# Two-part weights of a mixer kept in DRAM by its first block, and elementwise work moved from GpSimd to VectorE

## The chip, the core and the metric

The kernel runs on one core of a Trainium2 chip. Its engines work side by side: TensorE (PE in the rows; PEld is its weight load) multiplies, VectorE (DVE), ScalarE (ACT) and GpSimd (POOL) work elementwise, SyncE (SP) issues all DMA transfers of this kernel from one queue, in order, and 16 DMA engines carry them out. The metric is device time of one execution in microseconds. Before the change the median of three runs is 2590.94 us (2590.84 to 2595.94).

## What is computed

One layer of a streaming encoder on 2048 tokens of width 1024, in float32. Cut to what matters:

```python
def _token_mixer(xn, w_in, ..., w_out):
    p = einsum('btd,de->bte', xn, w_in)
    gB, gC, hA = split(p[..., :3 * CONV_DIM], 3)
    y_a = gC * _causal_dwconv(gB * hA, conv_a_w)
    ...                                # r, k, v, decay, gate of a delta-rule state
    y = _wkv7(r4, d4, k4, v4, kk, a4)  # chunks of 64 tokens, one after the other
    ...
    return einsum('bte,ed->btd', concatenate([y_a, y_b]), w_out)

def _channel_mixer(hn, w_up, ffn_conv_w, ffn_conv_b, w_down):
    f = einsum('btd,df->btf', hn, w_up)
    f = _causal_dwconv(f, ffn_conv_w) + ffn_conv_b
    gate, up = split(f, 2)
    return einsum('btf,fd->btd', gelu(gate) * up, w_down)

h = x + rms_norm(_token_mixer(rms_norm(x, pre_mix_g), ...), post_mix_g)
out = h + rms_norm(_channel_mixer(rms_norm(h, pre_ffn_g), ...), post_ffn_g)
```

## The kernel before

The 2048 tokens are four blocks of 512. **Operands in two parts.** TensorE multiplies in float32r, so every weight and every activation is split into a high part (`hi`, a cast by ScalarE) and a low part (`lo = src - hi`, a subtraction by VectorE): `split`, line 483. A product is three matmuls, high by high, high by low, low by high. `gemm` (line 490) does that for one output tile of 128 columns: it takes the weights in pieces of 128x512 (256 KB, four 128-row tiles, 12 matmuls), loads a piece into the ring `wraw` (three buffers), and splits it into the rings `whi` and `wlo` (three buffers each). Half of an input projection of 1024 rows is one piece.

**Mixer weights met four times.** The input weights `w_in` are used by all four blocks. For them `gemm` gets a name `keep`: block 0 computes both parts and stores the low one to DRAM (`lower`), blocks 1 to 3 load the raw piece, cast `hi` again on ScalarE, and load `lo`. In block 0 the low part of the second piece (k0 = 4) is computed by GpSimd (`pool_e if keep and k0 else dve`). This holds for 26 projections, 52 pieces. The output weights `w_out` (8 tiles, 16 pieces) are split anew in each of the four calls of `out_proj` (line 599), on ScalarE and VectorE.

**Stages.** The mixer blocks 0 to 3 (each a plan of its own) mix projections with the chain of the 64-token state; block b also does `out_proj(b-1)` and `residual`. Then one plan holds the rest: `out_proj(3)`; `up(0)` for blocks 0 and 1 (22 pairs of tiles, seven half-size products each, after Strassen's scheme, in `up_pair`), where `up_weights` also forms four sums of weight quarters and stores them (`s_d`); `down_block(0)` and `down_block(1)`; `up(1)` for blocks 2 and 3, which loads the stored sums; `down_block(2)` and `(3)`. Of the four sums, s1 and s3 (`wu0s`, `wu2s`) run on GpSimd, s2 and s4 (`wu1s`) on VectorE.

**Other GpSimd work.** In block 0 `short_conv` multiplies by the late norm factor (`u`, `cv`). At the end of each down block `finish` (line 1497) scales the eight tiles `fo` by the norm factor and adds the residual `ho` to them: tiles 0 to 2 are scaled and tiles 0 and 1 added by GpSimd, which needs a copy `rb` of the factor that ScalarE takes out of PSUM; VectorE does the others, straight from PSUM (`rps`). `ho` has two buffers, so tile 2 is loaded when tile 0 has been stored. The operand `t4` of `up(1)` lies in the places of `fo` (slots 48 to 55), so its last part is written when `finish(1)` is through.

**What sets the order.** Nothing runs in the order of the code. The code records operations into a `Plan`, which schedules them as a list, engine by engine, by costs of its own (`Plan.cost`, a price for each kind of operation, engine and width) over 16 rounds, and then emits them; on the chip each engine and the one DMA queue keep that order. All instructions are recorded by one helper, so the profile gives line 431 for all, and one goes by tile names.

## Time and profile before

| | us |
|---|---|
| median of three runs | 2590.94 |
| lowest, highest | 2590.84, 2595.94 |
| the profiled execution, whole | 2591.45 |
| its span, first to last instruction | 2589.7 |

In that span TensorE is busy 2479.0 us (96%), VectorE 2025.0 (78%), ScalarE 1476.6 (57%), GpSimd 152.8 (6%), and the DMA engines move 432.29 MB, a mean of 167 GB/s. A share of busy time is a mean over stages with different limits; so the page is read first by stage, then by what TensorE waited for in each.

### The profile page before, as it was taken

Reading aid. Unit: us, or ns where it says so; the run is one execution under the profiler, and the core shown is the slowest. Engines: PE = TensorE matmul, PEld = TensorE weight load, DVE = VectorE, ACT = ScalarE, POOL = GpSimd, SP = SyncE. Lnnn points to the kernel's source line nnn. Section 1 sums busy time; section 2 is a strip of 40 time slices with the busy share of each in tenths; the row PEclk is TensorE's granted clock in tenths of the full one; section 3 lists DMA queues with packets and bytes.
Section 4 is the critical chain, followed back from the end, with each engine's and each line's share of the span. In section 5 each row is a group of like instructions: output and inputs, shape, how many; then the busy total and the mean of one; then the engine's idle time right before and its main releaser. Section 6 shows DMA issues by size and latency. Waiting matters only on the chain.

```text
span 2589.7 us, 41292 instructions
## 1 busy us (share of the span) xinstructions
PE 2479.0 (96%) x14210; PEld 1948.8 (75%) x14210; DVE 2025.0 (78%) x4159; ACT 1476.6 (57%) x3070; POOL 152.8 (6%) x116
## 2 busy tenths in 40 slices
PE   8988999999999899989999999999989999999997
PEld 6766777777786677667877778788868888888886
DVE  7989878889786889768999999855478787784534
ACT  7555766566656555456656566543456666673532
POOL 1311000000000000001111121001010000000001
PEclk9999999999999899989999999999999999999998
DMA  6535454557454675465464634775654444454653
GB/s 204 175 100 167 130 172 131 165 163 257 130 171 148 203 248 163 150 202 179 154 192 147 202 131 167 249 247 172 190 183 126 122 118 130 120 160 130 191 183 106
DMA packets 239970, 432.29 MB, mean 167 GB/s; under 512 B 26640, under 2 KB 33424, under 8 KB 239760
## 3 DMA queue, kind: packets, MB, share of 16 engines
q1 hardware_dynamic: 239760, 429.65, 52.7%
q8 instruction: 112, 1.84, 0.3%
q14 instruction: 98, 0.80, 0.1%
HBM read 321.54 MB, written 108.00 MB: 166 GB/s over the span
## 4 chain that ended last, share of the span: by engine, by line
PE 64%; DVE 20%; DMA 8%; issue 4%; ACT 4%; SPq 0%; POOL 0%; DVEq 0%; ACTq 0%; POOLq 0%
PE dn L431 17%; PE upa L431 13%; PE upc L431 6%; PE op L431 5%; PE upb L431 3%; PE rp_ps L431 3%; PE kp_ps L431 2%; PE pc L431 2%; DVE cv L431 2%; PE vp_ps L431 2%; PE ch_ps L431 2%; PE cb_ps L431 1%; PE cc_ps L431 1%; DVE gt L431 1%; PE y L431 1%
## 5 line engine op out<-in xcount | busy, mean ns | idle before, releaser
L431 DVE TENSOR_TENSOR wd_l<-wd_r,wd_h 128x512 fp32r<-128x512 f32 x198 | 129.9, 658 | 200.0 <-ACT wd_h L431 190.9
L431 DVE SCALAR_TENSOR_TENSOR cv<-co,vec,cv 128x512 f32<-128x512 f32 x352 | 272.9, 800 | 13.5 <-ACT cv L431 12.1
L431 PE MATMUL dn<-gh,wd_h 128*128 128x512 f32 (+1 forms) x726 | 281.2, 388 | 0.9 <-ACT gh L431 0.6
L431 PE MATMUL dn<-gh,wd_l 128*128 128x512 f32 (+1 forms) x726 | 280.1, 386 | 0.2 <-DVE wd_l L431 0.2
L431 PE MATMUL dn<-gl,wd_h 128*128 128x512 f32 (+1 forms) x726 | 279.0, 384 | 0.2 <-DVE gl L431 0.2
L431 ACT ACTIVATE wd_h<-wd_r 128x512 fp32r<-128x512 f32 x198 | 117.4, 595 | 251.7 <-PE dn L431 220.4
L431 DVE SCALAR_TENSOR_TENSOR gt<-gt,cv 128x512 f32<-128x512 f32 x264 | 177.5, 694 | 2.0 <-ACT gt L431 0.8
L431 ACT ACTIVATE cv<-co,vec 128x512 f32<-128x512 f32 x176 | 142.3, 811 | 44.2 <-DVE co L431 35.4
L431 PEld LDWEIGHTS dn<-gl,wd_h 128*128 128x128 f32 x726 | 136.3, 188 | 30.2 <-DVE gl L431 1.3
L431 PEld LDWEIGHTS dn<-gh,wd_l 128*128 128x128 f32 x726 | 136.4, 188 | 30.0 <-DVE wd_l L431 0.4
L431 PEld LDWEIGHTS dn<-gh,wd_h 128*128 128x128 f32 x726 | 136.4, 188 | 29.3 <-ACT gh L431 1.7
L431 ACT ACTIVATE wua_h<-wua 128x512 fp32r<-128x512 f32 x132 | 82.6, 626 | 82.1 <-issue 38.4
L431 PE MATMUL op<-y_h,wo_h 128*128 128x512 f32 x256 | 101.6, 406 | 5.3 <-ACT y_h L431 4.2
L431 PE MATMUL op<-y_l,wo_h 128*128 128x512 f32 x256 | 102.4, 404 | 0.6 <-DVE y_l L431 0.4
L431 PE MATMUL op<-y_h,wo_l 128*128 128x512 f32 x256 | 101.7, 402 | 0.2
L431 DVE TENSOR_TENSOR wua_l<-wua,wua_h 128x512 fp32r<-128x512 f32 x132 | 96.9, 735 | 4.8 <-ACT wua_h L431 4.7
L431 ACT ACTIVATE wus_h<-wus 128x512 fp32r<-128x512 f32 x88 | 55.6, 632 | 68.2 <-PE upa L431 25.2
L431 DVE TENSOR_TENSOR ut<-nt,um 128x120 f32<-128x120 f32 (+24 forms) x248 | 70.0, 282 | 5.4
L431 DVE TENSOR_TENSOR um<-um,ut 128x120 f32<-128x120 f32 (+24 forms) x248 | 70.1, 283 | 5.2
L431 POOL TENSOR_TENSOR fo<-fo,fn_rb 128x512 f32<-128x512 f32 (+1 forms) x15 | 17.7, 1197 | 941.9 <-ACT fn_rb L431 941.9
L431 DVE TENSOR_TENSOR gl<-gk,gh 128x512 fp32r<-128x512 f32 x88 | 59.0, 687 | 16.1 <-ACT gh L431 15.9
L431 ACT ACTIVATE gt<-cv 128x512 f32<-128x512 f32 x88 | 55.0, 625 | 25.4 <-DVE cv L431 24.6
(731 smaller groups left out, 7081.0 us busy)
## 6 DMA issues: line engine op xcount, KB each, us to landing
wd_r<-in_w_down SPq DMA_DIRECT2D x165, 256.0 KB, 2.8
wua<-in_w_up SPq DMA_DIRECT2D x154, 256.0 KB, 3.0
g_d<-gt SPq DMA_DIRECT2D x88, 256.0 KB, 2.6
gk<-g_d SPq DMA_DIRECT2D x88, 256.0 KB, 3.3
wus<-s_d SPq DMA_DIRECT2D x88, 256.0 KB, 3.2
wo_r<-in_w_out SPq DMA_DIRECT2D x64, 256.0 KB, 3.3
s_d<-wu1s SPq DMA_DIRECT2D x44, 256.0 KB, 3.1
x<-in_x_t SPq DMA_DIRECT2D x32, 256.0 KB, 4.2
```

Of the source, the lines that this page charges most:

```text
L431: getattr(getattr(self.nc, e), m)(*[real(a) for a in args], **{k: real(a) for k, a in kw.items()})
```

## The change

Four edits. **(1)** Block 0 stores both parts of each kept piece (`store_parts`), and the later blocks load both straight into `whi` and `wlo`: no raw load and no cast. **(2)** `w_out` gets a name too, so `out_proj(0)` stores its parts and calls 1 to 3 load them. **(3)** Every tensor_tensor of GpSimd goes to VectorE: the 26 low parts and 8 late factors of block 0, the 44 sums of `up(0)`, and 25 operations of the five calls of `finish`, 103 in all. **(4)** `finish` needs no copy `rb`, so `over_partitions` returns the PSUM tile when it is given no pool.

```diff
-    lower = {}
+    parts_d = {}
+
+    def store_parts(hi, lo, name):
+        there = [dram.tile([128, 4, 128], F32, name=f"{name}{p}") for p in "hl"]
+        for part, t in zip((hi, lo), there):
+            nc.sync.dma_start(out=t, in_=part.bitcast(F32))
+        return there
...
-            raw = wst.tile([128, 4, 128], F32, tag="wraw", name=f"{name}_r{k0}", bufs=WB[0])
-            nc.sync.dma_start(out=raw[:, 0:n, :], in_=src[:, k0:k0 + n, :])
             hi = wst.tile([128, 4, 128], F32R, tag="whi", name=f"{name}_h{k0}", bufs=WB[1])
             lo = wst.tile([128, 4, 128], F32R, tag="wlo", name=f"{name}_l{k0}", bufs=WB[1])
-            if (keep, k0) in lower:
-                act(hi, raw, AF.Copy)
-                nc.sync.dma_start(out=lo.bitcast(F32), in_=lower[keep, k0])
+            kept = parts_d.get((keep, k0))
+            if kept:
+                for part, there in zip((hi, lo), kept):
+                    nc.sync.dma_start(out=part.bitcast(F32), in_=there)
             else:
-                split(raw[:, 0:n, :], hi[:, 0:n, :], lo[:, 0:n, :],
-                      pool_e if keep and k0 else dve)
+                raw = wst.tile([128, 4, 128], F32, tag="wraw", name=f"{name}_r{k0}", bufs=WB[0])
+                nc.sync.dma_start(out=raw[:, 0:n, :], in_=src[:, k0:k0 + n, :])
+                split(raw[:, 0:n, :], hi[:, 0:n, :], lo[:, 0:n, :], dve)
                 if keep:
-                    lower[keep, k0] = dram.tile([128, 4, 128], F32, name=f"{keep}_l{k0}")
-                    nc.sync.dma_start(out=lower[keep, k0], in_=lo.bitcast(F32))
+                    parts_d[keep, k0] = store_parts(hi, lo, f"{keep}_{k0}")
...
-            gemm(ps, w_out[d], KT, xs, f"wo{b}_{d}")
+            gemm(ps, w_out[d], KT, xs, f"wo{b}_{d}", f"wo{d}")
...
-                    pool_e.tensor_tensor(out=u[:, 2:TB + 2], in0=u[:, 2:TB + 2], in1=late,
-                                         op=ALU.mult)
+                    dve.tensor_tensor(out=u[:, 2:TB + 2], in0=u[:, 2:TB + 2], in1=late,
+                                      op=ALU.mult)
...
-                    pool_e.tensor_tensor(out=cv, in0=cv, in1=late, op=ALU.mult)
+                    dve.tensor_tensor(out=cv, in0=cv, in1=late, op=ALU.mult)
...
-                engine.tensor_tensor(out=o, in0=a, in1=b, op=op)
+                dve.tensor_tensor(out=o, in0=a, in1=b, op=op)
...
-                rb, rps = over_partitions(rf, nm, o1, "nrb", both=True, n=n)
+                rps = over_partitions(rf, nm, None, "nrb", n=n)
...
-                    if d < 3:
-                        pool_e.tensor_tensor(out=fd, in0=fd, in1=rb, op=ALU.mult)
-                    else:
-                        dve.tensor_tensor(out=fd, in0=fd, in1=rps, op=ALU.mult)
-                    (pool_e if d < 2 else dve).tensor_tensor(out=hk, in0=fd, in1=hk, op=ALU.add)
+                    dve.tensor_tensor(out=fd, in0=fd, in1=rps, op=ALU.mult)
+                    dve.tensor_tensor(out=hk, in0=fd, in1=hk, op=ALU.add)
```

Since the plan is made anew, every engine's order changes. Three places follow; a name's trailing number is a buffer's, `x0_7` is tile 7 of block 0's input, `wi3_4l` the stored low part of the second piece of projection 3.

The DMA queue (SP) in the first microseconds of block 0, before:

```order
L431 DMA x0_3_148<-in_x_t 128x512
L431 DMA kp0_0_r4_162<-in_w_in 128x512
L431 DMA wi0_l0_167<-wa0_l0_154 128x512
L431 DMA x0_4_171<-in_x_t 128x512
L431 DMA x0_5_189<-in_x_t 128x512
L431 DMA vp0_0_r4_194<-in_w_in 128x512
L431 DMA wi3_l0_201<-kp0_0_l0_184 128x512
L431 DMA vp0_0_r0_212<-in_w_in 128x512
L431 DMA wi0_l4_216<-wa0_l4_196 128x512
L431 DMA x0_6_220<-in_x_t 128x512
L431 DMA rp0_0_r0_240<-in_w_in 128x512
L431 DMA x0_7_246<-in_x_t 128x512
```

and now:

```order
L431 DMA wi0_0h_163<-wa0_h0_154 128x512
L431 DMA kp0_0_r4_173<-in_w_in 128x512
L431 DMA wi0_0l_178<-wa0_l0_165 128x512
L431 DMA x0_5_185<-in_x_t 128x512
L431 DMA wi3_0h_191<-kp0_0_h0_175 128x512
L431 DMA wi0_4h_198<-wa0_h4_182 128x512
L431 DMA vp0_0_r4_205<-in_w_in 128x512
L431 DMA wi3_0l_210<-kp0_0_l0_188 128x512
L431 DMA vp0_0_r0_216<-in_w_in 128x512
L431 DMA wi0_4l_224<-wa0_l4_200 128x512
L431 DMA x0_6_230<-in_x_t 128x512
L431 DMA x0_7_238<-in_x_t 128x512
```

The stores of the high parts (`0h`, `4h`) stand between the loads; ahead of the last input tile `x0_7` there were 20 transfers and there are 22.

The DMA queue in the last output projection (`wo3_d`: weights of tile d; `xr...`: operands of `up(0)`; `mix_d3`: results), before:

```order
L431 DMA wo3_3_r0_13181<-in_w_out 128x512
L431 DMA wo3_4_r0_13191<-in_w_out 128x512
L431 DMA xrb11_01_13203<-xr0b111_10803 128x512
L431 DMA xrb11_02_13212<-xr0b112_11064 128x512
L431 DMA xrb11_03_13219<-xr0b113_11729 128x512
L431 DMA mix_d3_13232<-ov3_0_13223 128x512
L431 DMA wo3_3_r4_13237<-in_w_out 128x512
L431 DMA mix_d3_13232<-ov3_1_13235 128x512
L431 DMA wo3_4_r4_13251<-in_w_out 128x512
L431 DMA xrt1_00_13261<-xr0t10_10692 128x512
L431 DMA xrt1_01_13275<-xr0t11_10917 128x512
```

and now:

```order
L431 DMA wo3_2_h0_12987<-wo2_0h_5642 128x512
L431 DMA wo3_2_l0_12995<-wo2_0l_5664 128x512
L431 DMA mix_d3_13001<-ov3_0_12992 128x512
L431 DMA xrb11_03_13005<-xr0b113_11554 128x512
L431 DMA wo3_3_h0_13008<-wo3_0h_5670 128x512
L431 DMA wo3_3_l0_13012<-wo3_0l_5681 128x512
L431 DMA mix_d3_13001<-ov3_1_13010 128x512
L431 DMA xrt1_00_13024<-xr0t10_10562 128x512
L431 DMA xrt1_01_13033<-xr0t11_10785 128x512
L431 DMA wo3_3_h4_13047<-wo3_4h_5727 128x512
L431 DMA wo3_3_l4_13051<-wo3_4l_5751 128x512
```

Each raw load of a piece has become two loads, of its high and its low part.

VectorE at the end of `finish(1)`, beside the first pair of `up(1)` (`b22`, `t4`: operands; `wus`, `wua`: weights; `co`: its sums), before:

```order
L431 TENSOR_TENSOR b22_10l_20390<-xrb22_10_20334,b22_10h_20379 128x512
L431 TENSOR_TENSOR fo1_3_19726<-fo1_3_19726,fn1_0_ps_20381 128x512
L431 TENSOR_TENSOR fo1_4_19838<-fo1_4_19838,fn1_0_ps_20381 128x512
L431 TENSOR_TENSOR fo1_5_20006<-fo1_5_20006,fn1_0_ps_20381 128x512
L431 TENSOR_TENSOR b22_11l_20414<-xrb22_11_20358,b22_11h_20405 128x512
L431 TENSOR_TENSOR wus41_0_l_20419<-wus41_0_20166,wus41_0_h_20392 128x512
L431 TENSOR_TENSOR fo1_6_20142<-fo1_6_20142,fn1_0_ps_20381 128x512
L431 TENSOR_TENSOR b22_12l_20439<-xrb22_12_20388,b22_12h_20422 128x512
L431 TENSOR_TENSOR b22_13l_20443<-xrb22_13_20397,b22_13h_20436 128x512
L431 TENSOR_TENSOR fo1_7_20281<-fo1_7_20281,fn1_0_ps_20381 128x512
L431 TENSOR_TENSOR wua221_0_l_20460<-wua221_0_20176,wua221_0_h_20428 128x512
L431 TENSOR_TENSOR wua111_1_l_20468<-wua111_1_20172,wua111_1_h_20454 128x512
```

GpSimd at the same place before (it has nothing there now):

```order
L431 TENSOR_TENSOR fo1_0_19381<-fo1_0_19381,fn1_0_rb_20400 128x512
L431 TENSOR_TENSOR fo1_1_19504<-fo1_1_19504,fn1_0_rb_20400 128x512
L431 TENSOR_TENSOR ho1_0_19849<-fo1_0_19381,ho1_0_19849 128x512
L431 TENSOR_TENSOR ho1_1_19853<-fo1_1_19504,ho1_1_19853 128x512
L431 TENSOR_TENSOR fo1_2_19618<-fo1_2_19618,fn1_0_rb_20400 128x512
```

VectorE now:

```order
L431 TENSOR_TENSOR b22_10l_20148<-xrb22_10_20092,b22_10h_20137 128x512
L431 TENSOR_TENSOR fo1_0_19136<-fo1_0_19136,fn1_0_ps_20139 128x512
L431 TENSOR_TENSOR fo1_1_19260<-fo1_1_19260,fn1_0_ps_20139 128x512
L431 TENSOR_TENSOR ho1_0_19607<-fo1_0_19136,ho1_0_19607 128x512
L431 TENSOR_TENSOR ho1_1_19611<-fo1_1_19260,ho1_1_19611 128x512
L431 TENSOR_TENSOR fo1_2_19376<-fo1_2_19376,fn1_0_ps_20139 128x512
L431 TENSOR_TENSOR fo1_3_19484<-fo1_3_19484,fn1_0_ps_20139 128x512
L431 TENSOR_TENSOR b22_11l_20186<-xrb22_11_20116,b22_11h_20158 128x512
L431 TENSOR_TENSOR fo1_4_19596<-fo1_4_19596,fn1_0_ps_20139 128x512
L431 TENSOR_TENSOR fo1_5_19764<-fo1_5_19764,fn1_0_ps_20139 128x512
L431 TENSOR_TENSOR co101_0_19954<-upa1_0_20014,m51_0_20109 128x512
```

The scaling and adding of tiles 0 and 1 stands at once behind `b22_10l` on VectorE, where before the scaling of tile 3 stood.

## Rows read from the trace of the kernel before

**Rows 1.** By stage: us; PE, PEld, DVE, ACT, POOL busy (count); clock; DMA share; GB/s.

```profile
0.00:240.00 240.00, 209.47 (x1381) 158.58 (x1382) 210.60 (x459) 143.69 (x322) 47.43 (x44) 0.97 0.48 155
240.00:1110.00 870.00, 843.40 (x6578) 636.42 (x6578) 712.83 (x1912) 527.15 (x1204) 2.39 (x2) 0.99 0.54 173
1110.00:1185.00 75.00, 65.69 (x285) 51.36 (x285) 51.37 (x105) 43.79 (x86) 3.07 (x3) 0.89 0.69 222
1185.00:1618.00 433.00, 419.44 (x1809) 336.08 (x1808) 411.23 (x637) 269.19 (x548) 69.59 (x42) 0.99 0.49 164
1885.00:2320.00 435.00, 423.01 (x1827) 342.31 (x1826) 351.52 (x552) 268.39 (x512) 8.09 (x5) 0.99 0.46 135
2320.00:2590.00 270.00, 253.54 (x1179) 209.12 (x1177) 130.98 (x241) 103.09 (x183) 15.28 (x15) 0.97 0.51 155
```

**Rows 2.** Instruction groups, 1183 to 1618 us: shapes, count, busy us, mean ns, idle before.

```profile
L431 DVE SCALAR_TENSOR_TENSOR cv<-co,vec,cv 128x512 f32<-128x512 f32 x165 | 138.2, 859 | 4.1 <-ACT cv L431 3.4
L431 DVE TENSOR_TENSOR wua_l<-wua,wua_h 128x512 fp32r<-128x512 f32 x63 | 49.3, 783 | 1.6 <-ACT wua_h L431 1.6
L431 POOL TENSOR_TENSOR wu2s<-wua,wua 128x512 f32<-128x512 f32 x21 | 35.2, 1676 | 139.0 <-DVE wus_l L431 139.0
L431 DVE TENSOR_TENSOR wu1s<-wu0s,wua 128x512 f32<-128x512 f32 x21 | 14.3, 682 | 3.8 <-POOL wu0s L431 3.8
```

**Rows 3.** The same view, 1940 to 2310 us, where GpSimd is idle.

```profile
L431 DVE SCALAR_TENSOR_TENSOR cv<-co,vec,cv 128x512 f32<-128x512 f32 x154 | 110.5, 748 | 8.3 <-ACT cv L431 7.6
L431 DVE TENSOR_TENSOR wua_l<-wua,wua_h 128x512 fp32r<-128x512 f32 x58 | 39.7, 684 | 0.0
```

**Rows 4.** Waits of the DMA queue (SPq), 0 to 240 us: total, times, longest.

```profile
SPq L431 <- POOL ch_l L431: 18.9, 4, 12.6
```

**Rows 5.** By stage again: first 20 us, last output projection, start of second up-projection.

```profile
0.00:20.00 20.00, 12.10 (x41) 8.26 (x42) 12.05 (x20) 14.82 (x27) 6.02 (x15) 1.00 0.87 279
1140.00:1170.00 30.00, 29.44 (x130) 23.93 (x129) 20.30 (x32) 21.09 (x37) 0.00 (x0) 1.00 0.93 306
1895.00:1930.00 35.00, 23.01 (x80) 14.92 (x78) 28.28 (x41) 16.16 (x31) 5.87 (x4) 0.85 0.63 204
```

**Rows 6.** Instruction groups of ScalarE, 240 to 1110 us.

```profile
L431 ACT ACTIVATE kp_h<-kp_r 128x512 fp32r<-128x512 f32 x24 | 15.0, 626 | 11.5 <-PE cb_ps L431 4.2 <-PE op L431 2.0 <-PE gb_ps L431 1.6
```

**Rows 7.** The chain that ended last, mixer blocks: start us, us, what.

```profile
349.48 5.44 PE ch_ps L431 x24
```

**Rows 8.** DMA issues, 810 to 1110 us: count, size, median us to landing.

```profile
vp_l<-wi_l SPq DMA_DIRECT2D x8, 256.0 KB, 3.4
```

**Rows 9.** Waits of TensorE, 240 to 1110 us.

```profile
PE vp_ps L431 <- DMA vp_l<-wi_l: 1.3, 2, 0.8
PE cb_ps L431 <- DMA cb_l<-wi_l: 1.2, 1, 1.2
```

**Rows 10.** Waits of TensorE, 1185 to 1618 us.

```profile
PE upa L431 <- ACT m L431: 6.0, 6, 3.4
PE hn_tsum L431 <- DVE hacc L431: 2.9, 1, 2.9
```

**Rows 11.** The chain, 1860 to 1935 us.

```profile
1895.76 1.75 POOL ho L431
1899.75 0.60 DVE fo L431
1903.67 4.00 DMA ho<-h_d
1922.41 0.64 ACT t_13h L431
```

**Rows 12.** Instructions of VectorE in order of time, last 28 us.

```profile
2571.56 1.42 DVE L431 TENSOR_TENSOR fo<-fo,fn_ps 128x256 f32<-128x256 f32 x4 [0.45 <-ACT fn_rb L431]
2572.89 3.41 DVE L431 TENSOR_TENSOR ho<-fo,ho 128x256 f32<-128x256 f32 x5
2584.63 1.63 DVE L431 TENSOR_TENSOR ho<-fo,ho 128x256 f32<-128x256 f32 x3
```

More of the change, by code (lines that the diff above doesn't have):

```diff
@@ L542, in inv_rms, with over_partitions @@
         rsqrt(o1, ms, [128, n], name, out=out)
-    def over_partitions(y, name, pool, tag, bufs=1, both=False, n=4):
+    def over_partitions(y, name, pool, tag, bufs=1, n=4):
         dg = o1.tile([128, 4, 128], F32, tag="sq", name=f"{name}_dg")
@@ L554, in over_partitions @@
                                  start=True, stop=True)
+        ps = ps[:, 0:n * 128]
+        if pool is None:
+            return ps
         rb = pool.tile([128, TB], F32, tag=tag, name=f"{name}_rb", bufs=bufs)[:, 0:n * 128]
-        ps = ps[:, 0:n * 128]
         act(rb, ps, AF.Copy)
-        return (rb, ps) if both else rb
+        return rb
     def token_sums(accs, name, n=4):
@@ L1340, in parts, with summed @@
                 return hi, lo
-            def summed(a, b, op, j, engine, o=None):
+            def summed(a, b, op, j, o=None):
                 plan.rank = R_WEIGHT
@@ L1355, in up_weights @@
                 yield parts(a11, "a11")
-                s1 = summed(a21, a22, ALU.add, 0, pool_e)
+                s1 = summed(a21, a22, ALU.add, 0)
                 yield parts(s1, "s1")
-                s2 = summed(s1, a11, ALU.subtract, 1, dve)
+                s2 = summed(s1, a11, ALU.subtract, 1)
                 yield parts(s2, "s2")
                 yield parts(a12, "a12")
-                s3 = summed(a11, a21, ALU.subtract, 2, pool_e)
+                s3 = summed(a11, a21, ALU.subtract, 2)
                 yield parts(s3, "s3")
-                s4 = summed(a12, s2, ALU.subtract, 3, dve, s2)
+                s4 = summed(a12, s2, ALU.subtract, 3, s2)
                 yield parts(s4, "s4")
```

## The prediction

> **What bounds the kernel now.** I read the busy times by stage first: in each row the first number is the stage's length and the second TensorE's busy time; their difference is TensorE's idle time. It is 30.5 us of 240 in block 0, 26.6 of 870 in blocks 1 to 3, 9.3 of 75 in `out_proj(3)`, 13.6 of 433 in `up(0)`, 12.0 of 435 in `up(1)`, 16.5 in the last 270 [rows 1]. TensorE bounds the kernel, and the change takes no matmul away: it can gain only in those 108 us, and it loses where it makes a new gap. VectorE comes next: 411.23 us of 433 (95%) in `up(0)` and 210.60 of 240 in block 0, where GpSimd works, but 351.52 of 435 (81%) in `up(1)` [rows 1]. Second I read the instruction groups of the two up-projections side by side, where the same instruction stands beside a busy and an idle GpSimd [rows 2, 3]; third the densest short stretches for DMA [rows 5]; last the waits and the chain at the places that the change touches.
>
> **What the move to VectorE costs.** GpSimd's sum takes 1676 ns; the same shape on VectorE has a mean of 682 ns beside it [rows 2], and a link of the chain takes 0.60 us [rows 11]. I take 0.60. In `up(0)` 42 sums move: 42 x 0.60 = 25.2 us more on VectorE. Against it, two kinds of VectorE instruction are slower there than in `up(1)`: `cv` 859 against 748 ns, 165 times, 18.3 us; `wua_l` 783 against 684, 63 times, 6.2 us [rows 2, 3]. That is 24.5 us given back for 69.59 us of GpSimd [rows 1], 0.35 us for each. So VectorE's own time in `up(0)` hardly changes. By the same ratio block 0 gets 32 x 0.60 = 19.2 us more and 47.43 x 0.35 = 16.6 back: +2.6 us on an engine that is busy for 210.60 of 240.
>
> The Trainium skill (SBUF — State Buffer, "Who interferes with whom") says that VectorE and GpSimd share a port pair as an exclusive lock. The slower rows agree in sign, and their 0.35 us is far from all of GpSimd's time. If every us of GpSimd held VectorE up, `up(0)` would be like `up(1)`, its term below -7.3 instead of -5, and the sum 2.3 us lower.
>
> **Start of block 0.** In the first 20 us the DMA engines are busy at 0.87 and TensorE for 12.10 us [rows 5]. The last input tile now has 22 transfers ahead instead of 20. One of 256 KB costs 0.80 us there: 306 GB/s at a share of 0.93 is 329 GB/s at full share [rows 5]. Two make **+1.6 us** (0 to +4: the norm of the block waits for that tile; at the upper end five stores come between).
>
> **Rest of block 0.** 52 stores are added, 41.6 us of DMA time on a share of 0.48 over 240 us [rows 1], so they fit. The queue no longer stands for GpSimd, which computed the low parts that it stores: `ch_l` alone held it for 18.9 us [rows 4]. The wait of a store for its part stays, but it is VectorE's now, shorter, in the same in-order queue with loads behind it. VectorE's +2.6 us speaks against. I take **0** (-4 to +5: a quarter of what `ch_l` held, either way).
>
> **Blocks 1 to 3.** Of `w_in` two transfers a piece stay two. Each loses its cast on ScalarE, 0.626 us [rows 6]: 156 of them and the 48 of `w_out` are 128 us. VectorE loses 48 low parts, about 33 us at 684 ns [rows 3]. Neither is the bound (VectorE 712.83 and ScalarE 527.15 of 870 [rows 1]), so they count only through the 26.6 us in which TensorE is idle. Against it: both parts now come by DMA into rings of three. 24 matmuls take 5.44 us [rows 7], so a piece's 12 take 2.72, and a place in the ring is released two pieces, 5.4 us, before its next use must begin. A stored part lands 3.4 us after its issue [rows 8]; with a second one behind it 4.2. That leaves 1.2 us. The low parts have come through such a ring all along, and TensorE waited for them 2.5 us in 3 of 156 loads [rows 9]. The traffic of `w_out`, 32 stores and 32 loads, adds 51 us of DMA time to a share of 0.54 over 870. I take **0** (-5 to +6): up, the 2.5 us more than double; down, a fifth of the idle time.
>
> **out_proj(3).** 16 more loads are 12.8 us of DMA time. The stage has a share of 0.69 of 75 us, 23 us free, but its middle runs at 0.93 with TensorE busy for 29.44 of 30 us [rows 1, 5]. Most of the loads can go ahead or into the gap. I take **+2** (0 to +8, when two thirds of the 12.8 come late).
>
> **up(0).** Of 13.6 us idle, 2.9 belong to the residual's sum and 3.4 to one wait at the start [rows 10], which the change leaves; 7.3 are waits for PSUM to be emptied. In `up(1)`, with the same work and no GpSimd, all 12.0 us lie in its first 35 us [rows 1, 5]: none is left of that kind. There VectorE is at 81%, here it will stay near 95%. But the sum's 1.68 us, for which VectorE waited (3.8 us [rows 2]), becomes 0.60, and evacuations no longer stretch. Between -7.3 and 0 I take **-5**, nearer to `up(1)`, the same products; the range reaches to +2, since the two sides of VectorE's balance come from different stretches.
>
> **Start of up(1).** TensorE is busy for 23.01 of the 35 us from 1895, at a granted clock of 0.85 [rows 5]; that is the 12.0 us. The chain goes through GpSimd's adding of `ho` (1.75 us), the store, a load of the next `ho` (4.00 us), and the rest of `finish(1)`, to the part of the operand `t4` that takes the places of `fo` (1922.41) [rows 11]. GpSimd's first four instructions, 4 x 1.75 = 7.0 us, become 4 x 0.60 = 2.4 at the head of VectorE's queue, and the wait for the copy `rb` goes, by the cast's 0.63 us [rows 6]. **-5.2** (-8 to -2): the rounds of 4.00 us through two buffers stay and are late next, and VectorE, 28.28 of 35 busy, takes five instructions more.
>
> **Tail.** The two slices of the last `finish` each lose a wait of 0.45 us for the copy, and the five adds that took 3.41 us beside GpSimd go at 1.63/3 = 0.54 each, 0.7 us less [rows 12]. Against it five instructions more stand in the last slice's row on VectorE, 5 x 0.45 = 2.2 us, part of them beside stores. **0** (-2 to +2).
>
> **Sum.** 1.6 + 0 + 0 + 2 - 5 - 5.2 + 0 = -6.6 us. The profiled execution took 2591.45, which gives 2584.8; from the median of 2590.94 it gives 2584.3. I say **2585**. The terms' bounds, added as independent errors, give 2577 to 2598 for this case.
>
> **Rivals.** *A: the gain is given back.* VectorE is as full in `up(0)` as before, so TensorE's waits stay (0 instead of -5): 2590. Or the DMA terms come to their upper ends, +4 and +8 instead of 1.6 and 2: 2593. For it speaks the balance of 25.2 against 24.5; against it the empty rest of `up(1)`. *B: slower, since the parts come late in blocks 1 to 3.* Before, a raw piece could wait in a ring of its own ahead of the cast; now only three places of `whi` and `wlo` hold what is loaded ahead. It decides when the second part lands over 5.4 us after its place is released: 3.4 us and three transfers of 0.80 ahead of it are 5.8, so two foreign ones between suffice, and the stores of `w_out` and of the state's tiles share the queue. If one piece in eight of 156 waits 1.2 us, the longest in [rows 9], that is 23 us, less some 3 that ScalarE's relief gives: 2605. Against it: the low parts were in that position, at 2.5 us. *C: slower, since VectorE takes the work and gets no relief.* If `cv` stays over 800 ns, under half of the 24.5 us comes back; with none, `up(0)` needs 436.4 us of VectorE and, with as little idle time as TensorE has now, 450: +17 instead of -5, 2607, and block 0 can add to it. Against it: [rows 2, 3] differ in nothing else as plainly as in GpSimd. That the change doesn't do what it says is no rival: the order of the changed kernel has the two loads and the moved instructions.
>
> **How the numbers follow.** A measurement of this kernel tells 0.2%, 5.2 us, from no change: below 2585.8 counts as faster, above 2596.1 as slower. Forecast 0.55 (0.43 of it faster, 0.12 within, as its middle lies near the bound), A 0.23, B 0.14, C 0.08. Faster 0.43, same 0.35, slower 0.22. The range goes from 2572, a little past the forecast's own, since a newly made order may close more of the idle time than the rows tell, to 2606, with most of B in it.
>
> **What would show it.** Right: `cv` in `up(0)` near 750 ns and VectorE still near 411 us there; `up(0)`'s TensorE idle time at 7 to 10 us; 7 us idle in the start of `up(1)` instead of 12.0, with `t_13h` some 5 us earlier; waits of TensorE for loads of parts below 6 us in blocks 1 to 3; `out_proj(3)` at a share near 0.85. Wrong: dozens of waits of TensorE for `wi` loads (B), `cv` above 800 ns (C), TensorE's idle time in `up(0)` still 13 (A), or a new order that opens gaps in the state's chain in blocks 1 to 3, which no row here tells.

## The result

The changed kernel takes 2550.56 us in the median (four runs, 2546.22 to 2552.68) against 2593.44 before: a ratio of 0.9832, 95% interval 0.9811 to 0.9852. It is faster by about 43 us. The forecast was 2585 us, in a range of 2572 to 2606: the sign was right, but the sum of -6.6 us was six and a half times too small, and 2550.56 lies below the stated range.

One statement ahead of the prediction is not right: the four mixer blocks are not a plan each. They are recorded into one plan, which is run behind the loop over the blocks. An edit in block 1 can therefore change the order in block 0, and the experiments below have to be read with that.

The stages of the two kernels, cut where the first projection of block 1, the end of `out_proj(2)`, the first pair of `up(0)`, the first tile of `down_block(0)`, the first pair of `up(1)` and the first tile of `down_block(2)` stand on TensorE. Columns as in [rows 1]; before:

```profile
0.00:242.50 242.50, 211.97 (x1393) 160.65 (x1393) 213.10 (x463) 144.50 (x323) 48.52 (x45) 0.97 0.49 156
242.50:1115.50 873.00, 846.40 (x6601) 638.59 (x6599) 714.27 (x1926) 529.32 (x1213) 1.30 (x1) 0.99 0.54 172
1115.50:1178.80 63.30, 53.99 (x218) 41.91 (x218) 41.87 (x71) 36.67 (x69) 2.19 (x3) 0.87 0.72 234
1178.80:1630.30 451.50, 437.06 (x1892) 350.45 (x1891) 427.75 (x668) 283.00 (x576) 70.47 (x43) 0.99 0.50 166
1630.30:1880.60 250.30, 248.65 (x1087) 202.07 (x1086) 141.84 (x234) 108.14 (x192) 6.95 (x5) 1.00 0.68 214
1880.60:2331.00 450.40, 438.41 (x1898) 355.03 (x1897) 366.18 (x577) 280.39 (x535) 8.09 (x5) 0.99 0.47 138
2331.00:2589.70 258.70, 242.54 (x1131) 200.08 (x1129) 120.02 (x224) 94.61 (x166) 15.28 (x15) 0.97 0.50 152
```

After, the same stages:

```profile
0.00:229.70 229.70, 212.83 (x1409) 163.60 (x1409) 203.84 (x480) 143.30 (x320) 2.06 (x12) 0.97 0.65 221
229.70:1097.90 868.20, 844.22 (x6593) 638.96 (x6591) 705.63 (x1913) 431.04 (x1032) 0.00 (x0) 0.99 0.59 192
1097.90:1164.10 66.20, 53.82 (x209) 41.07 (x210) 28.84 (x53) 27.11 (x49) 0.17 (x1) 0.90 0.85 294
1164.10:1592.20 428.10, 427.26 (x1886) 349.91 (x1885) 417.37 (x709) 286.64 (x574) 0.00 (x0) 1.00 0.53 175
1592.20:1840.70 248.50, 248.50 (x1094) 203.18 (x1093) 145.33 (x242) 108.17 (x193) 0.00 (x0) 1.00 0.69 217
1840.70:2288.60 447.90, 438.08 (x1898) 355.96 (x1897) 366.05 (x583) 279.66 (x534) 0.00 (x0) 0.99 0.47 139
2288.60:2544.40 255.80, 242.56 (x1131) 200.33 (x1129) 120.99 (x239) 92.95 (x163) 0.00 (x0) 0.98 0.51 154
```

Two stages carry the gain: `up(0)` goes from 451.5 us to 428.1, and block 0 from 242.5 to 229.7. Blocks 1 to 3 go from 873.0 to 868.2, `out_proj(3)` gets longer (63.3 to 66.2, at a DMA share of 0.85 instead of 0.72), and the three stages behind `up(0)` give 7 us together. In `up(0)` TensorE's idle time falls from 14.4 us to 0.8, and its busy time falls as well, from 437.06 to 427.26, though the work is the same.

What answers to [rows 2] in `up(0)` of the changed kernel (instruction groups: shapes, count, busy us, mean ns, idle before):

```profile
L431 DVE SCALAR_TENSOR_TENSOR cv<-co,vec,cv 128x512 f32<-128x512 f32 x168 | 122.0, 745 | 1.3 <-ACT cv L431 1.1
...
L431 DVE TENSOR_TENSOR wua_l<-wua,wua_h 128x512 fp32r<-128x512 f32 x64 | 43.7, 683 | 0.2 <-ACT wua_h L431 0.2
...
L431 DVE TENSOR_TENSOR wu0s<-wua,wua 128x512 f32<-128x512 f32 x21 | 14.4, 686 | 0.1
L431 DVE TENSOR_TENSOR wu2s<-wua,wua 128x512 f32<-128x512 f32 x21 | 14.4, 685 | 0.1
```

`cv` and `wua_l` stand at 745 and 683 ns, as in [rows 3], and a sum's row on VectorE lasts 0.69 us (back to back, instructions of this size start 0.60 us apart there, the prediction's figure). And what answers to [rows 10], TensorE's waits in that stage (total, times, longest):

```profile
PE upa L431 <- ACT u L431: 0.8, 2, 0.4
```

That is the only row left: the waits for `m`, and for `hacc` too, are gone.

### The profile page after: what moved, and what is told of

Read it like the earlier page. It is cut to its first block, busy times and chain, and to the rows that moved or that the text cites. A ratio compares the mean times of both kernels' runs of the same rounds, so it can differ in the third digit from the quotient of the medians.

```text
span 2544.4 us, 41039 instructions
## 1 busy us (share of the span) xinstructions
PE 2467.3 (97%) x14210; PEld 1953.0 (77%) x14210; DVE 1988.1 (78%) x4214; ACT 1368.9 (54%) x2861; POOL 2.2 (0%) x13
## 5 line engine op out<-in xcount | busy, mean ns | idle before, releaser
L431 DVE SCALAR_TENSOR_TENSOR cv<-co,vec,cv 128x512 f32<-128x512 f32 x352 | 254.2, 747 | 10.7 <-ACT cv L431 9.8
L431 DVE TENSOR_TENSOR wua_l<-wua,wua_h 128x512 fp32r<-128x512 f32 x132 | 90.3, 684 | 3.5 <-ACT wua_h L431 3.3
L431 ACT ACTIVATE sv<-sn,pct 64x64 f32<-64x64 f32 x112 | 32.5, 336 | 79.5 <-DVE sn L431 78.9
L431 PEld LDWEIGHTS op<-y_h,wo_h 128*128 128x128 f32 x256 | 48.5, 191 | 27.4 <-ACT y_h L431 9.5
L431 ACT ACTIVATE gh<-gk 128x512 fp32r<-128x512 f32 x88 | 54.9, 627 | 26.5 <-DMA gk<-g_d 24.2
L431 DVE TENSOR_TENSOR ut<-nt,um 128x120 f32<-128x120 f32 (+24 forms) x248 | 64.8, 261 | 5.3
```

The source lines that it names most:

```text
L431: getattr(getattr(self.nc, e), m)(*[real(a) for a in args], **{k: real(a) for k, a in kw.items()})
```

## The experiments

A table holds what all runs say of place. For each kernel it has the time by which TensorE has done the same amount of matmul work, less the time of the kernel before: near the end of block 0, at the end of the mixer blocks, at the end of `up(0)`, and at the end. (The work is counted from the trace's matmul rows, each at the usual pitch of its kind.) The points lie at about 273, 1150, 1700 and 2560 us of the kernel before. So the difference of the second and third column is what `up(0)` gains or loses. Each row is one profiled execution. Two kernels stand there twice, and their rows differ by up to 5.2 us (7.0 at the end); the column of block 0 moves by up to 5 us when its point is moved between 200 and 273 us. A difference of under some 5 us between two rows of these columns says nothing. The last two columns are the medians against runs of the kernel before on the same chip.

```
kernel         block 0   mixers    up(0)      end   ratio    95% interval
after            -11.5    -15.5    -39.9    -42.2   0.9832   0.9811-0.9852
after_2          -13.7    -20.3    -42.6    -43.5   0.9816   0.9800-0.9831
e_moves          -12.5     -4.0    -27.0    -31.8   0.9854   0.9839-0.9869
e_parts           +3.0     +6.0     +5.5     +7.4   1.0013   1.0004-1.0022
e_sums            -1.2     -1.5    -23.5    -21.6   0.9909   0.9894-0.9925
e_block0         -11.0     -5.6     -5.7     -2.4   0.9972   0.9961-0.9984
a_dummy          -14.5    -16.7    -10.9    -13.2   0.9931   0.9911-0.9950
a_dummy_tiny     -12.9    -14.7    -37.2    -40.3   0.9815   0.9800-0.9830
a_sums_pool      -14.5    -20.2    -17.4    -20.1   0.9904   0.9888-0.9920
a_no_wout        -15.3    -18.6    -42.5    -43.7   0.9799   0.9785-0.9814
a_no_wout_2      -16.9    -18.0    -37.3    -36.7   0.9802   0.9782-0.9822
e_win             +3.3     -1.7     -1.9     +0.8   0.9992   0.9983-1.0002
b_dummy           +2.1    +12.5    +13.8    +16.0   1.0020   1.0010-1.0030
b_late           -11.7     -7.9     -8.9     -7.7   0.9952   0.9937-0.9967
a_late            -7.8     -4.8    -25.6    -28.8   0.9856   0.9841-0.9871
o_late           -14.0    -10.3     -8.5     -6.9   0.9962   0.9948-0.9976
c_recast          -1.3     -0.0    -23.8    -23.6   0.9887   0.9858-0.9916
o_before          +4.6     +1.5     +1.6     +4.4   1.0003   0.9993-1.0013
o_no_wout        -14.6    -13.0    -35.8    -34.1   0.9820   0.9798-0.9842
```

### Which edit

**e_moves**: the kernel before with every GpSimd operation on VectorE.

```diff
-                      pool_e if keep and k0 else dve)
+                      dve)
...
-                    pool_e.tensor_tensor(out=cv, in0=cv, in1=late, op=ALU.mult)
+                    dve.tensor_tensor(out=cv, in0=cv, in1=late, op=ALU.mult)
...
-                s1 = summed(a21, a22, ALU.add, 0, pool_e)
+                s1 = summed(a21, a22, ALU.add, 0, dve)
...
-                rb, rps = over_partitions(rf, nm, o1, "nrb", both=True, n=n)
+                rps = over_partitions(rf, nm, None, "nrb", n=n)
```

> The kernel before with all 103 tensor_tensor operations of GpSimd on VectorE and finish without its copy; the input weights keep raw load, cast and stored low part, the output weights are split anew. Theory G (GpSimd's place in the work was the cost, by its hold on VectorE and by its own slowness): nearly all of the gain, 2550 to 2558 us, with 15 us won in the rest of block 0 and 23 us in up(0). Rival P (the stored parts and ScalarE's relief bring it): 2580 us or more. Rival O (any newly made order gives some gain): somewhere between, with gains in other stages than block 0 and up(0).

Measured: 2557.61 us, 37 us under the kernel before. By the table 23 us of that are in `up(0)` and 12.5 in block 0, but 8.5 are lost again in blocks 1 to 3. **e_parts** is the other half, the stored parts without the moves:

```diff
+                split(raw[:, 0:n, :], hi[:, 0:n, :], lo[:, 0:n, :],
+                      pool_e if keep and k0 and not keep.startswith("wo") else dve)
                 if keep:
-                    lower[keep, k0] = dram.tile([128, 4, 128], F32, name=f"{keep}_l{k0}")
-                    nc.sync.dma_start(out=lower[keep, k0], in_=lo.bitcast(F32))
+                    parts_d[keep, k0] = store_parts(hi, lo, f"{keep}_{k0}")
```

> The kernel before with both parts of the input and output weights stored and loaded; GpSimd keeps the low parts of the second pieces in block 0, the late factors, the sums and its part of finish. Theory G: within 6 us of the kernel before, with a loss of 2 to 4 us at the start and of 2 us in out_proj(3), and at most 6 us won in blocks 1 to 3. Rival P: 2560 to 2570 us, the gain in blocks 1 to 3. Rival O: a shift of 5 to 15 us either way, at no place that the edit touches.

Measured: 2598.24 us, 3 us slower than before, ratio 1.0013 (1.0004 to 1.0022). By itself the part of the change that takes 128 us off ScalarE brings nothing. Theory G holds for the bulk.

**e_sums** and **e_block0** take the moves apart: only `s1` and `s3` of `up(0)`, and only the 26 low parts and 8 late factors of block 0.

```diff
-                s1 = summed(a21, a22, ALU.add, 0, pool_e)
+                s1 = summed(a21, a22, ALU.add, 0, dve)
...
-                s3 = summed(a11, a21, ALU.subtract, 2, pool_e)
+                s3 = summed(a11, a21, ALU.subtract, 2, dve)
```

> The kernel before with only the 42 to 44 sums s1 and s3 of up(0) on VectorE. Theory G: up(0) becomes 20 to 24 us shorter, 2567 to 2572 us in all, nothing else moves. Rival P: up(0) stays within 5 us, as the prediction's term had it. Rival O: a gain in up(0) that is not repeated where GpSimd's work comes back under the changed kernel's order.

Measured: 2570.96 us, 24 us less, by the table all of it in `up(0)` (-1.5 to -23.5). Two lines of code are more than half of the whole gain. The stage, in the columns of [rows 1]:

```profile
1177.30:1606.50 429.20, 427.96 (x1885) 349.51 (x1884) 417.61 (x708) 284.78 (x573) 0.00 (x0) 1.00 0.52 173
```

```diff
-                      pool_e if keep and k0 else dve)
+                      dve)
...
-                    pool_e.tensor_tensor(out=u[:, 2:TB + 2], in0=u[:, 2:TB + 2], in1=late,
-                                         op=ALU.mult)
+                    dve.tensor_tensor(out=u[:, 2:TB + 2], in0=u[:, 2:TB + 2], in1=late,
+                                      op=ALU.mult)
...
-                    pool_e.tensor_tensor(out=cv, in0=cv, in1=late, op=ALU.mult)
+                    dve.tensor_tensor(out=cv, in0=cv, in1=late, op=ALU.mult)
```

> The kernel before with only the 26 low parts and 8 late factors of block 0 on VectorE. Theory G: block 0 becomes 12 to 19 us shorter, 2574 to 2580 us in all; the DMA queue's waits for GpSimd's low parts are gone. Rival P: block 0 within 4 us of before, as VectorE has 2.6 us more to do there. Rival O: part of the gain is lost again in blocks 1 to 3.

Measured: 2588.74 us, not the 2574 to 2580 of theory G: 7 us are left. By the table block 0 is 11 us shorter, a little less than theory G's 12 to 19; some 5 us of it seem to go again in blocks 1 to 3, as rival O said, and 3 behind `up(0)`, but these two are no larger than the table's own uncertainty.

### What GpSimd does to up(0)

The sums can have cost time in two ways: GpSimd holds VectorE up, or the weights wait for a slow sum. **a_dummy** leaves all sums on VectorE and gives GpSimd additions that nobody reads; **a_dummy_tiny** does the same on 128x4.

```diff
+        idle = f1.tile([128, 4, 128], F32, tag="ho", name="idle", bufs=2)
+        pool_e.memset(idle, 0.0)
...
                 dve.tensor_tensor(out=o, in0=a, in1=b, op=op)
+                if j in (0, 2):
+                    pool_e.tensor_tensor(out=idle[:, :, 0:128], in0=idle[:, :, 0:128],
+                                         in1=o[:, :, 0:128], op=ALU.add)
```

> The changed kernel with 44 more GpSimd additions of 128x512 in up(0), one beside each sum s1 and s3, into a tile that nobody reads; VectorE keeps all sums. Theory K (GpSimd's hold on VectorE is the cost): cv in up(0) goes from 745 back to 840 ns or more, VectorE runs over its 428 us, and 15 to 23 us are lost, 2565 to 2575 us. Theory L (it was GpSimd's slow sum for which the chain of weights waited): within 4 us of the changed kernel, though cv gets longer. Both: in between, with each one's part readable from up(0) alone.

Measured: 2577.42 us, 27 and 32 us more than the changed kernel's two results (2550.56, and 2545.66 in after_2 below), and more than the 15 to 23 of theory K. `up(0)` of a_dummy, in the same views as above:

```profile
1164.00:1620.30 456.30, 436.86 (x1886) 346.45 (x1885) 452.11 (x707) 283.68 (x573) 89.14 (x43) 1.00 0.49 164
```

```profile
L431 DVE SCALAR_TENSOR_TENSOR cv<-co,vec,cv 128x512 f32<-128x512 f32 x167 | 139.3, 853 | 1.3 <-ACT cv L431 1.2
...
L431 DVE TENSOR_TENSOR wua_l<-wua,wua_h 128x512 fp32r<-128x512 f32 x64 | 47.7, 745 | 0.4 <-ACT wua_h L431 0.2 <-issue 0.2
...
L431 POOL TENSOR_TENSOR idle<-idle,wu0s 128x512 f32<-128x512 f32 x21 | 32.5, 1546 | 205.0 <-DVE wu0s L431 205.0
```

The stage takes 456.3 us, longer than in the kernel before. VectorE has the instructions of the changed kernel and is busy for 452.11 us instead of 417.37, 99% of the stage; `cv` is back at 853 ns. The 34.7 us are 0.39 us for each of GpSimd's 89.14, close to the 0.35 of the prediction.

> The same with additions of 128x4 in place of 128x512: the same instructions and dependences, hardly any data. Theories K and L: within 4 us of the changed kernel. If it loses as much as its larger companion, the order of the plan or the dependences were the cause, not GpSimd's accesses.

Measured: 2548.36 us, no loss. Its rows:

```profile
1165.30:1595.00 429.70, 427.93 (x1886) 349.62 (x1886) 417.67 (x709) 287.19 (x574) 58.64 (x43) 1.00 0.52 174
```

```profile
L431 DVE SCALAR_TENSOR_TENSOR cv<-co,vec,cv 128x512 f32<-128x512 f32 x168 | 124.2, 762 | 1.3 <-ACT cv L431 1.2
...
L431 POOL TENSOR_TENSOR idle<-idle,wu0s 128x4 f32<-128x4 f32 x21 | 9.8, 467 | 194.8 <-DVE wu0s L431 194.8
```

Same instructions and dependences, 429.7 us. In `up(0)` VectorE and TensorE have their instructions in the same order in the changed kernel, in a_dummy and in a_dummy_tiny, but for a few places. So it is GpSimd's data, not its instructions, their order or their semaphores. **a_sums_pool** puts the two sums back into the changed kernel (the diff of e_sums, reversed):

> The changed kernel with the sums s1 and s3 of up(0) back on GpSimd. If the up(0) gain is the sums' alone, whatever stands before: 20 to 25 us lost, 2571 to 2576 us. If it hangs on the new order of the blocks ahead: under 12 us lost.

Measured: 2569.66 us, 19 to 24 us more than the changed kernel's two results. The gain of `up(0)` is there whatever stands ahead of it: the nine runs of the table whose GpSimd does nothing in `up(0)` win 19 to 24 us there (after, after_2, e_moves, e_sums, a_no_wout, a_no_wout_2, a_late, c_recast, o_no_wout), and a_dummy_tiny 22; those in which it adds whole tiles gain at most 1 us there, or lose up to 5.8.

Two limits of this have to be said. In e_sums VectorE's order in `up(0)` is another one than before, so that run alone doesn't part the order from the hold; a_dummy does. And a_dummy shows that the hold is enough to make the loss, but not that the slow sum (theory L) cost nothing: VectorE carries the sums there as well, beside 89 us of GpSimd instead of 70, and before the change it stood for `wu0s` for 3.8 us in all [rows 2]. Scaled by GpSimd's time the 28.2 us that a_dummy loses in the stage are 22.3 for 70.47 us of GpSimd, against the 23.4 won: an estimate, which leaves little for L.

What the hold looks like is seen in block 0 of the kernel before, on VectorE in order of time:

```profile
121.08 1.40 DVE L431 TENSOR_TENSOR um<-um,ut 128x144 f32<-128x144 f32 x1
122.51 1.27 DVE L431 TENSOR_TENSOR ut<-nt,um 128x136 f32<-128x136 f32 x1
123.82 0.30 DVE L431 TENSOR_TENSOR um<-um,ut 128x136 f32<-128x136 f32 x1
...
127.70 1.76 DVE L431 TENSOR_TENSOR rp_l<-rp_r,rp_h 128x512 fp32r<-128x512 f32 x1
```

and GpSimd:

```profile
120.48 1.84 POOL L431 TENSOR_TENSOR cv<-cv,x_rb 128x512 f32<-128x512 f32 x1 [1.26 <-issue]
122.27 1.35 POOL L431 TENSOR_TENSOR vp_l<-vp_r,vp_h 128x512 fp32r<-128x512 f32 x1
127.63 1.29 POOL L431 TENSOR_TENSOR rp_l<-rp_r,rp_h 128x512 fp32r<-128x512 f32 x1 [4.00 <-ACT rp_h L431]
```

A link `ut` or `um` of the state's chain takes 0.30 us. One that meets GpSimd stands until GpSimd's instruction is through: `um` from 121.08 ends at 122.48, GpSimd's `cv` at 122.32; `ut` from 122.51 ends at 123.78, GpSimd's `vp_l` at 123.62; `rp_l` on VectorE, usually 0.68, takes 1.76 us and ends 0.54 behind GpSimd's. A mean over a group hides this. Counted over single rows of `up(0)` before, 35 VectorE instructions last over 0.25 us longer than is usual for their group. Each lies beside one of GpSimd's sums, about one for each sum, and stands for 0.9 us more: 31.4 us together (36.5 in a_dummy). After the change, in e_sums and in a_dummy_tiny there is none. So one instruction stands for about a us, and behind it the whole in-order queue.

### Block 0

**b_dummy** adds 26 unread GpSimd additions to e_block0, one for each second piece.

```diff
                     nc.sync.dma_start(out=lower[keep, k0], in_=lo.bitcast(F32))
+                    if k0:
+                        if not spare:
+                            spare.append(o1.tile([128, 4, 128], F32, tag="ov", name="idle", bufs=2))
+                            pool_e.memset(spare[0], 0.0)
+                        pool_e.tensor_tensor(out=spare[0][:, :, 0:128], in0=spare[0][:, :, 0:128],
+                                             in1=hi[:, :, 0:128].bitcast(F32), op=ALU.add)
```

> The kernel before with block 0's 34 operations on VectorE, and 26 more GpSimd additions of 128x512 in block 0 that nobody waits for, one at each second piece. Theory K (GpSimd's hold on VectorE is the cost there too): block 0 is again 8 to 15 us longer than with the 34 operations moved alone. Theory L (the weights and the DMA queue waited for GpSimd's late results): block 0 keeps its gain within 3 us, since VectorE was not the bound there at every moment.

Measured: 2601.14 us, 12 us over e_block0, and 13 in block 0 by the table. So unread work of GpSimd costs there too, by the hold or by the order that was made anew with it. **b_late** moves only the 8 late factors (the second and third piece of e_block0's diff, not the first) and leaves the 26 low parts on GpSimd:

> The kernel before with only the 8 late factors of block 0 on VectorE; the 26 low parts stay with GpSimd. If GpSimd's hold on VectorE makes the loss, 8 of 34 operations bring about a quarter of block 0's 11 us: 2 to 4 us. If a single long wait on a GpSimd result (the late factor in the way of the state's chain) made it: 8 us or more.

Measured: 2583.99 us, and block 0 is 11.7 us shorter: all that e_block0 has. So moving the 26 low parts was worth nothing that these runs can tell, which is what the balance of the prediction gave for them (hold taken away against work added: 26 unread additions cost 13 us in b_dummy, and 26 operations at 0.60 us are 15.6 on VectorE); the 8 factors were worth the whole. The DMA queue still stands for GpSimd's low parts in b_late, 16.0 us for `cc_l` and 10.8 for `ch_l`, and block 0 is as short all the same. **o_late** is b_late with 9 rounds of the planner (`ROUNDS = 9`) instead of 16:

> The kernel before with the late factors on VectorE, made with 9 rounds of the planner in place of 16. If the 8 factors bring the 11 us of block 0 under any order: block 0 is 8 to 14 us shorter than in the kernel before here too. If the gain was one of order: under 4 us.

Measured: 2585.79 us, block 0 shorter by 14.0. **a_late** puts the 8 factors back on GpSimd in the changed kernel (the same two pieces, reversed):

> The changed kernel with the 8 late factors of block 0 back on GpSimd, which has nothing else there now. If the late factors on GpSimd hold block 0 by themselves (a long link in the chain of the convolution): 8 to 12 us lost in block 0, 2555 to 2560 us. If they were late only because GpSimd's low parts stood ahead of them in its queue, or if the order made the gain: under 4 us lost.

Measured: 2557.53 us, 7 and 12 us over the changed kernel's two results; by the table block 0 is only 3.7 us longer (0 to 5, by where the point is set), and the rest is lost in the blocks behind. So in block 0 the 8 factors cost 12 us beside GpSimd's other work and about 4 alone, while in the whole they cost nearly as much as b_late gained. The smaller figure fits a wait behind the low parts in GpSimd's queue, but in the rows above the factor `cv` at 120.48 us did not stand behind a low part. The hold has a share: from 110 to 128 us six VectorE instructions stand for about a us each, 6.1 us in all, two of them beside late factors and four beside low parts, and then TensorE waits 6.8 us for VectorE's `sc`; in b_late four stand, 4.3 us, and that wait is 4.1. But it is 5.5 in a_late with 2.0 us of holds, and 3.5 in c_recast with GpSimd idle, so the order has a share too. By what way the 12 us come is not shown.

### The stored parts, and the order

**a_no_wout** is the changed kernel with `w_out` split anew in each call, run twice, the second time beside the changed kernel (**after_2**) on the same chip.

```diff
-            gemm(ps, w_out[d], KT, xs, f"wo{b}_{d}", f"wo{d}")
+            gemm(ps, w_out[d], KT, xs, f"wo{b}_{d}")
```

> The changed kernel without the stored parts of the output weights: they are split anew in each call. If their 16 more loads cost out_proj(3) some 2 us and nothing else: 2547 to 2550 us. If the relief of VectorE (48 low parts) and ScalarE (48 casts) is what brings the last 7 us over the kernel with the GpSimd edits alone: 2555 to 2558 us. If that came from the input weights' parts: within 3 us of the changed kernel.

> The changed kernel again, to stand beside the next one on the same chip: 2546 to 2553 us, 0.981 to 0.985 of the kernel before.

> The changed kernel without the stored parts of the output weights, again, beside the whole. If these parts really cost time: 3 to 8 us under the changed kernel in this comparison too. If the first difference was the chip's: within 2 us of it.

Measured: 2543.12 the first time; then 2542.57 beside 2545.66. It is the fastest kernel of the study, 0.9799 and 0.9802 of the kernel before, but the 3 us between the two on one chip lie within their intervals: the stored parts of `w_out` bring nothing, and whether they cost something is not settled.

**e_win** is e_parts with this same line taken back:

> The kernel before with only the two stored parts of the input weights; GpSimd keeps all its work, low parts of the second pieces included, and the output weights are split anew. If those parts are worth the 14 us between the kernel with the GpSimd edits alone (2557.6) and the changed kernel without the output weights' parts (2543.1): 2577 to 2583 us. If they are worth that only once GpSimd no longer computes what the queue has to store: 2588 to 2597 us.

Measured: 2593.45 us, 0.9992 (0.9983 to 1.0002): nothing. Yet a_no_wout is 14 us faster than e_moves, from which it differs by just these parts. **c_recast** asks whether the casts made that: it casts each loaded high part once more in place.

```diff
                     nc.sync.dma_start(out=part.bitcast(F32), in_=there)
+                act(hi, hi.bitcast(F32), AF.Copy)
```

> The changed kernel without the output weights' parts, in which each loaded high part is cast once more in place by ScalarE: 156 casts in blocks 1 to 3 between landing and matmul, as before the change. Theory P (the stored parts help by the casts that go): the 12 us that blocks 1 to 3 win over the kernel with the GpSimd edits alone are lost, 2553 to 2558 us. Theory O (another order fell better there, the casts had cover): within 4 us of 2543.

Measured: 2564.77 us, 22 us slower than a_no_wout. But most of them, 8 to 15 by where the point is set, stand in block 0, where the edit adds no instruction: there the order changed, and no run shows that it was the order alone. In blocks 1 to 3 the table gives 4.6 us (+1.3 against -3.3) for 156 casts, within its uncertainty. **o_before** and **o_no_wout** change nothing but the order, with 9 rounds of the planner:

```diff
-ROUNDS = 16
+ROUNDS = 9
```

> The kernel before, made with 9 rounds of its planner in place of 16: same work, another order. It measures what an order alone is worth: theory O says that the whole moves by 4 to 12 us, the most of it in the mixer blocks; if it moves by under 3 us, order alone explains none of the differences of this study.

> The same with the changed kernel without the output weights' parts: 9 rounds in place of 16. Theory O: 4 to 12 us slower or faster in the mixer blocks, up(0) unchanged at 428 to 430 us.

Measured: 2594.83 us, the same as before (+4.6 in block 0 and -3.1 in blocks 1 to 3 by the table, both within its uncertainty); and 2549.73 us, some 7 us over a_no_wout, with intervals that overlap (0.9798 to 0.9842 against 0.9785 to 0.9814). So another order alone moved the whole kernel by 0 to 7 us here. What the stored input weights are worth, anything from 0 us (e_win) to 14 (a_no_wout against e_moves), the runs do not settle.

## Why the prediction was wrong

**What bounds the kernel.** "TensorE bounds the kernel" was read from means, and the gain was capped by TensorE's idle time. In `up(0)` the step that fails is "it can gain only in those 108 us", 13.6 us of them in this stage: the stage became 23.4 us shorter. 13.6 us of TensorE's idle time went, all there was but 0.8, and 9.8 us of its busy time, which the prediction took for fixed. Seen from VectorE the 23.4 us are 10.4 of busy time and 13.0 of standing still. It is not VectorE's share by itself that stops TensorE: after the change VectorE is at 97% of the shorter stage, and TensorE waits 0.8 us. It is the single instructions that stand for a us in a queue that has no slack to make it up.

Of the 9.8 us of busy time 1.4 are six rows fewer, and some 3.3 are an estimate from two falls of TensorE's clock (0.05 of 32 and of 34 us); the rest is not traced. The falls lie in two stretches around the residuals, before:

```profile
1316.00:1348.00 32.00, 28.81 (x125) 22.98 (x124) 30.24 (x50) 16.81 (x36) 5.57 (x3) 0.95 0.64 213
1428.00:1462.00 34.00, 30.47 (x124) 24.02 (x124) 30.65 (x50) 20.83 (x43) 4.81 (x3) 0.95 0.76 244
```

After, around the residuals:

```profile
1304.00:1340.00 36.00, 35.57 (x160) 29.05 (x159) 35.98 (x67) 23.04 (x46) 0.00 (x0) 1.00 0.58 190
1416.00:1450.00 34.00, 33.95 (x157) 27.78 (x156) 33.43 (x59) 20.62 (x41) 0.00 (x0) 1.00 0.57 183
```

Before, TensorE stands for about 3 us at once in each (the 2.9 and the 3.4 of [rows 10]), and its granted clock falls to a mean of 0.95: 1.7 us behind the end of the second gap seven matmuls follow at a pitch of 0.43 us instead of 0.23, the lower of the clock's two levels (1.2 and 2.4 GHz). After, neither gap nor fall. So such a gap cost its own length and, by the same estimate, half as much again in slower matmuls.

**up(0), -5 against -23.** The failing step is the sentence "2.9 belong to the residual's sum and 3.4 to one wait at the start [rows 10], which the change leaves". The 3.4 was not at the start: the two stand at 1448 and 1335 us, beside the residuals, and the change did not leave them. In front of each VectorE itself stood for a load, of the second:

```profile
1447.94 0.75 DVE L431 SCALAR_TENSOR_TENSOR md<-md,vec,on_rb 128x512 f32<-128x512 f32 x1 [2.10 <-DMA md<-mix_d]
```

In e_sums, which moves nothing but the sums, both gaps are gone too (TensorE's longest wait in the stage is 1.0 us), but they are also gone in a_sums_pool, which has the sums on GpSimd and loses as much in shorter waits. So by what way these two hung on the sums is open. The price of the hold (24.5 us, 0.35 for each us of GpSimd) was near: 31.4 us counted row by row, and 0.39 in a_dummy. The balance erred to the cautious side: VectorE's busy time was forecast to stay and falls from 427.75 to 417.37. What was wrong was to infer from a nearly even balance that most waits stay: the stands of over a us went, and rival A, built on that inference, fell with them.

**Rest of block 0, 0 against about -14.** The start cost about 1 us, within its bounds: the first product that needs the norm begins at 33.67 us instead of 32.53. The stage as a whole is 12.8 us shorter, so the rest of it won about 14. The low parts were rightly weighed at nothing (b_late against e_block0). The 8 late factors, counted as 8 of 32 equal operations at 0.60 us, were the failing term: 12 us beside the rest of GpSimd's work, by b_late, by a way that stays open. The bounds of -4 to +5, taken from the DMA queue's wait for `ch_l`, were too narrow: in b_late that queue still waits and block 0 is as short. TensorE's loss had a row of its own that the prediction did not read: its longest waits in block 0 before and, where that wait stood, 120 to 140 us before and after:

```profile
PE rp_ps L431 <- DVE sc L431: 6.8, 1, 6.8
```

```profile
120.00:140.00 20.00, 13.21 (x62) 10.20 (x62) 19.00 (x54) 6.36 (x15) 4.43 (x3) 0.83 0.59 197
```

```profile
120.00:140.00 20.00, 20.00 (x90) 16.48 (x89) 19.28 (x67) 9.24 (x22) 0.00 (x0) 1.00 0.96 328
```

**Blocks 1 to 3, 0 against -4 to -7.** Within the bounds of -5 to +6 in the stage's rows (-4.8); by the table after_2 lies just below them. Rival B did not come: the parts land in time, and the waits for them are these (TensorE, 229.7 to 1097.9 us):

```profile
PE op L431 <- DMA wo_h<-wo_0h: 1.6, 2, 1.0
...
PE vp_ps L431 <- DMA vp_h<-wi_0h: 1.3, 1, 1.3
PE op L431 <- DMA wo_l<-wo_0l: 1.2, 2, 0.9
```

4.1 us in all, and 1.3 for an input weight; [rows 9] had 2.5. A stored part lands in 2.6 to 5.9 us (medians), `vp_l` in 2.9 and 3.6 against 3.4 in [rows 8].

**out_proj(3), +2 against +2.9.** Right in size in the profiled execution, with its cause in a row, the wait for a piece's high part. Whether it is there in every execution of the changed kernel is not shown.

```profile
PE op L431 <- DMA wo_h<-wo_0h: 3.3, 1, 3.3
```

**Start of up(1), -5.2 against -2.5.** The step itself came as forecast: `t_13h` stands 37.5 us behind the stage's first matmul instead of 41.8, 4.3 us earlier. TensorE got half of it, as it waits for that operand all the same:

```profile
PE upa L431 <- ACT t_13h L431: 5.0, 1, 5.0
```

**Tail, 0 against -0.7 to -3.** The stage is 2.9 us shorter. The last tile of `down_block(3)` ends 0.7 us earlier against the stage's start, and what follows it, which is what the term was about, takes 2.1 us less, at the edge of its bounds of -2 to +2.

**Rival C** fell at its own mark: `cv` at 745 ns. **The rule on the shared port** (the Trainium skill, SBUF — State Buffer, "Who interferes with whom": an exclusive lock) stood in the prediction as a side remark worth 2.3 us. The single rows bear it out in this form: a VectorE instruction that meets GpSimd's ends when GpSimd's is through (1.27 us instead of 0.30, beside 1.35), about one for each of GpSimd's sums. The rule told the sign; the price, 0.35 to 0.45 us for each us of GpSimd, comes from the rows, and so does what the prediction missed, that the price falls on a queue without slack.

## What to carry to other kernels

Where TensorE's short waits hang on another engine's in-order queue that is as full as VectorE's here (95%), an even balance of that engine's busy time is no forecast: ask which single instructions stand for a us, and what is queued behind them, and don't cap the gain by TensorE's idle time, since its busy time can fall too. Before pricing a move off GpSimd, look at single rows of VectorE beside GpSimd's, not at group means. And where a planner makes the order anew, measure an order that differs in nothing else before believing a difference of a few us in the stages it mixes: here the number of rounds alone moved the whole by 0 to 7 us.

## What the runs showed of the hardware

GpSimd's addition on 128x4 took 467 ns beside one sum and 2224 beside the other (21 and 22 times), while the one on 128x512 took 1546 and 2582; what the long ones waited for is not shown:

```profile
L431 POOL TENSOR_TENSOR idle<-idle,wu2s 128x4 f32<-128x4 f32 x22 | 48.9, 2224 | 215.5 <-DVE wu2s L431 215.5
```

It cost VectorE nothing: `cv` had 762 ns there and 764 in e_moves, where GpSimd had nothing to do in that stage. But in the changed kernel it had 745, and `gt<-gt,cv`, which GpSimd hardly touches, 684 ns there, 703 and 705 in those two: VectorE itself was 2 to 3% slower in some runs, so a mean that is to show GpSimd's hold is read beside one that can't.
